# Output weights split during attention, output blocks handed out at 17 queued steps, and a VectorE that waits for GpSimd's power

## The chip, the cores and the metric

The kernel runs on one core of one Trainium2 chip. The metric is the device time of one execution in microseconds. The core has five engines with instruction streams of their own: TensorE (PE, the matmuls; its weight loads are counted apart as PEld), VectorE (DVE), ScalarE (ACT), GpSimd (POOL), and SyncE (SP), whose queue issues all the DMA transfers of this kernel, in order. Each engine runs its instructions in the order in which the program wrote them, and waits on semaphores for what the others make.

## The reference, cut to what matters

One decoder block, for one sequence of 1024 tokens and a width of 1024, in float32. The core of it:

```python
mod = silu(c) @ w_ada + b_ada              # six vectors: shift, scale, gate, twice
h = rms_norm(x, g_attn_pre) * (1 + sc_a) + sh_a
proj = h @ w_in                            # 1024 -> 2304 columns: qa, ka, va, qb, kb, vb
oa = banded_attention(...)                 # 8 heads, 2 key heads, window 128, with sinks
ob = dilated_mixture_attention(...)        # 8 heads, three dilated windows, mixed by softmax weight
mixed = concat(rms_norm(oa, g_mix_a), rms_norm(ob, g_mix_b))
y = mixed @ w_out                          # 1024 x 1024
x = x + gt_a * rms_norm(y, g_attn_post)
h = rms_norm(x, g_mlp_pre) * (1 + sc_m) + sh_m
y = square(relu(h @ w_up)) @ w_down        # 1024 -> 4096 -> 1024
x = x + gt_m * rms_norm(y, g_mlp_post)
```

## The kernel before, in words

**Products.** The large matmuls run in a rounded float32 format, fp32r. To keep the precision, each operand is split into a high part (the rounded value) and a low part (the value less the high part), and one product takes three matmuls: high by high, low by high, high by low. The splitting is elementwise work on ScalarE (the high part) and VectorE or GpSimd (the low part). One such group of three matmuls of 128 x 128 by 128 x 512 is called a dense step here.

**Stages.** (1) Modulation and normalization of x, whose result goes, split, into one large tile `hw` of 8 slots, each with a high and a low row of 1024 columns. (2) The input projection in six units u = 0 to 5 of two token halves x and three column tiles c; each tile has 8 dense steps, one for each 128 rows k of the weight (`proj_mm`, matmul lines L866, L867, L869). (3) Attention, in items of heads and token blocks: scores (L1127 and L1182), masked maximum (L1146, L1197), exponential (L1153, L1202), division by the sum (L1158 on GpSimd), transposes of the probabilities (L1232, L1235), splitting of the transposed probabilities on ScalarE and VectorE (L1246, L1250), the product with the values (L1262 to L1267, L1274), the values' own preparation (L836, L844, L847), and the store of an item's output to DRAM (L1301). Attention starts while the projections run and lasts some time after them. (4) The output projection in 8 blocks of 128 tokens (`out_block`, tb = 0 to 7): load the attention output `o_sb` (L1423), split it (L1436, L1439), compute the mixers' norms (L1441 to L1462), 16 dense steps with w_out (L1478 to L1480), post-norm, gate and residual (L1493 to L1524), the second norm, whose scaled result `xn` (L1532) is transposed on TensorE (`px`, L1541) and brought out as the MLP's input `h2` (L1557 on ScalarE, L1560 on VectorE). (5) The MLP in a Strassen-like scheme of seven block products for each half (`product`, matmuls L1912 to L1914), for which sums of weight blocks and of h2 blocks are made on VectorE (`sum_S` L1801, `sum_T` L1843) and split (L1667 to L1676).

**`hw` in turn.** The tile `hw` first holds the split activations, then the split w_out (a slot for each 128 rows k of w_out), then the operand pairs of the MLP. A slot can take w_out once the last projection tile that reads it is through. The counter `r_wo` stands for free slots. In the kernel before, k's 128 columns lie in all slots of a token half, so four slots come free together, at the end of a half's last tile (u = 5, c = 2).

**w_out.** `load_wo` does this for k = 0 to 7: a load of 128 x 1024 floats into one of five shared stage buffers (`wo_st`, L1348; the counter `r_stg`), the high part on ScalarE straight into `hw` (L1353), the low part on VectorE (L1356) or, in two instructions, on GpSimd (L1361, L1362), as the planner finds cheaper. The gate's row `gate_a` (L1377) and the buffers of the output blocks are made in the space of the stage buffers once those have been read.

**The order.** The order on each engine is not written by hand. A planner (`Sched`) builds it when the kernel is built: it keeps an estimated clock for each engine, a queue of steps for each, and for TensorE several streams ("s" scores, "t" transposes, "dense" and so on), with estimated durations, dependencies, priorities and counters of free buffers. It repeatedly takes the step that can start first. Feeders put steps into the queues when a condition holds: `feed_proj` keeps the dense stream filled with projection tiles, `feed_s` the attention items, `feed_out` hands out output blocks:

```python
if tb < TB and st.att >= 42 + 2 * (tb // 2) and len(sc.pe.get("dense", [])) <= 10:
    out_block(tb)
```

A step that can run on either of two engines names both. Once the order stands, the engines follow it, and what the chip needs beyond the estimates shows as waiting.

**The norms.** `norm(col, dep)` in `out_block` makes 1/sqrt(mean square + eps) of one column: VectorE scales and adds (L1515, tile `rs_t`), GpSimd raises it to the power -1/2 (L1517, tile `st`). Each block has two: one for the post-norm (col 0) and one for the MLP's pre-norm (col 2). ScalarE's `xn` waits for the second.

## Time and profile before

| | before |
|---|---|
| median of 3 runs | 1146.05 us (1145.21 to 1146.7) |
| the profiled execution's own time | 1144.1 us |
| its span, from first to last instruction | 1142.2 us |
| mean granted TensorE clock | 0.991 |
| TensorE busy | 1113.5 us, 97% |
| VectorE busy | 819.3 us, 72% |
| ScalarE busy | 636.1 us, 56% |
| GpSimd busy | 267.8 us, 23% |

The profile comes from one execution. Its rows give times in microseconds from the first instruction; an instruction row names its start, its length, the engine, the line of the kernel, the operation, its tiles (written <- read) and sizes, and in brackets the time that the engine sat idle before it with the instruction, on another engine or DMA, that released it. Matmuls overlap in the pipeline: a matmul that shows 0.39 us of length is followed by the next 0.23 us later. The granted clock is the share of TensorE's full speed that the chip allowed in a stretch. The projections run until 376.65 us, the first matmul of an output block stands at 397.86, the first of the MLP between the last output blocks (514.75 is one of them), and the MLP lasts to the end.

### The profile page before, as it was taken

To read this page: it belongs to the slowest core of one execution; us is meant where nothing else is said; L and a number is where in the kernel's file an instruction comes from. 1 tells how busy PE (TensorE), PEld (TensorE's weight loads), DVE (VectorE), ACT (ScalarE), POOL (GpSimd) and SP (SyncE) were. 2 spreads that over 40 slices of the span, in tenths; PEclk is the share of its full clock that TensorE was granted. 3 is DMA by queue.
4 is the path that set the end of the run, shared out by engine and by line. 5 is a ranking of instruction groups with operands and counts; after the bars stand their busy time and mean duration, and the time that the engine had idled before them with its cause. 6 is when DMAs were issued, how large, how long until landed. Compare 5 with 4: busy or idle time off the path is not lost.

```text
span 1142.2 us, 15600 instructions
## 1 busy us (share of the span) xinstructions
PE 1113.5 (97%) x5417; PEld 925.2 (81%) x5417; DVE 819.3 (72%) x1378; ACT 636.1 (56%) x1101; POOL 267.8 (23%) x349
## 2 busy tenths in 40 slices
PE   8999999999999899998999999999999999999996
PEld 7788878888888687887888888888888888888885
DVE  7878666666667766668879664599644896537998
ACT  8868865464556755676675434553244733246542
POOL 2458867565743521112000000000000000000002
PEclk9999999999999899999999999999999999999998
DMA  9565545343423305555780168712469112584103
GB/s 351 187 208 164 164 155 168 136 155 125 141 77 133 127 26 186 185 202 217 284 310 19 56 230 292 280 41 70 152 245 331 55 56 86 202 304 164 37 19 148
DMA packets 90910, 185.29 MB, mean 162 GB/s; under 512 B 8400, under 2 KB 31056, under 8 KB 90832
## 3 DMA queue, kind: packets, MB, share of 16 engines
q1 hardware_dynamic: 90832, 184.30, 46.1%
q8 instruction: 43, 0.70, 0.2%
q14 instruction: 35, 0.29, 0.1%
HBM read 137.08 MB, written 28.31 MB: 145 GB/s over the span
## 4 chain that ended last, share of the span: by engine, by line
PE 77%; DVE 8%; ACT 4%; issue 4%; POOL 3%; DMA 3%; SPq 0%; DVEq 0%; POOLq 0%; ACTq 0%
PE mlp_ps L1913 17%; PE mlp_ps L1914 17%; PE mlp_ps L1912 17%; PE pj L866 4%; PE pj L869 4%; PE pj L867 4%; PE s_ps L1127 3%; PE o_ps L1262 2%; PE y_ps L1478 1%; PE pt_ps L1232 1%; PE y_ps L1479 1%; PE y_ps L1480 1%; PE pt_ps L1235 1%; DMA o_sb<-o_dram 1%; PE o_ps L1267 1%
## 5 line engine op out<-in xcount | busy, mean ns | idle before, releaser
L1912 PE MATMUL mlp_ps<-hw 128*128 128x512 f32 x896 | 349.8, 390 | 0.0
L1913 PE MATMUL mlp_ps<-hw 128*128 128x512 f32 x896 | 348.8, 389 | 0.0
L1914 PE MATMUL mlp_ps<-hw 128*128 128x512 f32 x896 | 348.8, 389 | 0.0
L1912 PEld LDWEIGHTS mlp_ps<-hw 128*128 128x128 f32 x896 | 168.5, 188 | 35.5 <-issue 0.5
L1913 PEld LDWEIGHTS mlp_ps<-hw 128*128 128x128 f32 x896 | 168.4, 188 | 35.2 <-issue 0.5
L1914 PEld LDWEIGHTS mlp_ps<-hw 128*128 128x128 f32 x896 | 168.4, 188 | 34.9
L1676 DVE TENSOR_TENSOR hw<-w,hw 128x1024 fp32r<-128x1024 f32 x96 | 114.7, 1222 | 95.5 <-ACT hw L1669 95.2
L1669 ACT CAST hw<-w 128x1024 fp32r<-128x1024 f32 x96 | 97.7, 1047 | 128.1 <-PE mlp_ps L1914 97.5
L2012 POOL TENSOR_TENSOR st<-st,nhalf 128x1 f32<-128x1 f32 x8 | 7.8, 977 | 598.5 <-DVE st L2010 598.5
L866 PE MATMUL pj<-hw,w_hl 128*128 128x512 f32 x240 | 102.9, 429 | 0.0
L869 PE MATMUL pj<-hw,w_hl 128*128 128x512 f32 x240 | 95.1, 396 | 0.0
L867 PE MATMUL pj<-hw,w_hl 128*128 128x512 f32 x240 | 94.9, 395 | 0.0
L1250 DVE TENSOR_TENSOR ph<-pt_ps,ph 128x512 fp32r<-128x512 f32 (+1 forms) x110 | 69.5, 648 | 32.9 <-ACT ph L1246 32.6
L1669 ACT CAST hw<-u 128x1024 fp32r<-128x1024 f32 x48 | 48.6, 1051 | 64.6 <-PE mlp_ps L1914 64.6
L1246 ACT CAST ph<-pt_ps 128x512 fp32r<-128x512 f32 (+1 forms) x110 | 59.0, 556 | 31.2 <-PE pt_ps L1235 26.1
L1153 ACT ACTIVATE p_sb<-p_sb,mn 128x128 f32<-128x128 f32 (+3 forms) x64 | 49.7, 777 | 38.7 <-DVE mn L1146 37.2
L1676 DVE TENSOR_TENSOR hw<-u,hw 128x1024 fp32r<-128x1024 f32 x48 | 57.1, 1221 | 18.2 <-ACT hw L1669 18.2
L1970 DVE TENSOR_TENSOR yacc<-yacc,mlp_ps 128x512 f32<-128x512 f32 x96 | 62.3, 685 | 3.3 <-PE mlp_ps L1914 3.3
L1158 POOL TENSOR_SCALAR p_sb<-p_sb,den 128x128 f32<-128x128 f32 (+3 forms) x64 | 48.6, 765 | 55.4 <-DVE den L1156 50.8
L1015 POOL TENSOR_TENSOR ada_acc<-ada_acc,wa_st 128x512 f32<-128x512 f32 x42 | 54.9, 1307 | 3.5
L869 PEld LDWEIGHTS pj<-hw,w_hl 128*128 128x128 f32 x240 | 45.4, 189 | 10.6
L1478 PE MATMUL y_ps<-hw,oh 128*128 128x512 f32 x128 | 52.0, 406 | 0.0
(206 smaller groups left out, 2015.8 us busy)
## 6 DMA issues: line engine op xcount, KB each, us to landing
hw<-s_dram SPq DMA_DIRECT2D x84, 512.0 KB, 4.2
wa_st<-in_w_ada SPq DMA_DIRECT2D x32, 512.0 KB, 4.3
w<-in_w_up SPq DMA_DIRECT2D x32, 512.0 KB, 4.9
w<-in_w_down SPq DMA_DIRECT2D x32, 512.0 KB, 7.0
s_dram<-hw SPq DMA_DIRECT2D x28, 512.0 KB, 3.4
qt<-hl SPq DMA_DIRECT2D x40, 256.0 KB, 2.6
w_st<-in_w_in SPq DMA_DIRECT2D x36, 256.0 KB, 2.9
x_sb<-in_x SPq DMA_DIRECT2D x16, 512.0 KB, 6.5
```

The source lines that it names most:

```text
L866: T.matmul(ps, w[:, 0, n], h[0], start=(k == 0), stop=False)
L867: T.matmul(ps, w[:, 1, n], h[0], start=False, stop=False)
L869: T.matmul(ps, w[:, 0, n], h[1], start=False, stop=(k == KC - 1))
L1246: A.copy(b["ph"][:, 0, :w], b["pt"][:, :w])
L1250: V.tensor_tensor(b["ph"][:, 1, :w], b["pt"][:, :w], b["ph"][:, 0, :w].bitcast(F32), ALU.subtract)
L1478: T.matmul(ps[:], b["oh"][:, k], wh[:, c0:c0 + 512], start=(k == 4 * m), stop=False)
L1669: A.copy(out[j][0], flat(src[j]))
L1676: V.tensor_tensor(out[j][1], flat(src[j]), out[j][0].bitcast(F32), ALU.subtract)
L1912: T.matmul(ps[m][:], sh, mh, start=starts and k == 0, stop=False, **kw)
L1913: T.matmul(ps[m][:], sh, ml_, start=False, stop=False, **kw)
L1914: T.matmul(ps[m][:], sl, mh, start=False, stop=k == 3, **kw)
L1970: e = op("DVE", t_dv(512), lambda: V.tensor_tensor(y(), y(), ps[m][:], ALU.add), [e, ml.e_y[tb, n]], gives=gives, prio=1)
```

## The change

It has five parts.

1. The layout of `hw` during the projections: k's columns of a token half lie in one slot, 4x + k // 2, as 512 contiguous columns. A slot is free once the last projection tile has done an odd step k, and `r_wo` is given one by one.
2. The chunks 4 to 7 of w_out are split during attention (`split_wo`, called by `feed_wo` as the projections pass 2.2, 3.0, 3.8 and 4.6 units): load into a stage buffer, high part on ScalarE into a second stage buffer, low part on VectorE in place, and two stores of 512 KB to DRAM. `load_wo` later brings them into `hw` by eight loads of 512 KB without any splitting. It still splits the chunks 0 to 3 itself, with the low part always on VectorE.
3. `feed_out` hands out a block with up to 17 dense steps queued, before 10.
4. `norm`: the planner's estimate for the power is 0.55 instead of 1.2 us for blocks 0 to 5. For the second norm of block 7, the scaling (VectorE), the power (GpSimd) and a one-column copy on VectorE that reads the power's result are one step, so that VectorE does nothing else while GpSimd works.
5. `t.a = h2`: the MLP's first half refers to the dictionary of h2 tiles itself, not to a copy, so that its steps can be queued before all the tiles exist.

In the order that results, GpSimd has six w_out instructions fewer; VectorE has three more low parts and one copy; ScalarE has as many w_out passes as before; SP has 16 more DMA instructions; a few steps that two engines can do have changed sides. TensorE has the same 5417 matmuls, and the same number from the last projection matmul to the first of the MLP. The first matmul of an output block has 19 more attention instructions ahead of it. In block 7, VectorE makes the h2 tiles from px (L1560) before the last sums `sum_T` (L1843); in the kernel before one such sum stood ahead of them.

```diff
@@ -677,8 +677,8 @@
     def mod_chunk(k, eg, half):
         t0, t1 = (0, TB) if half is None else (4 * half, 4 * half + 4)
         n = (t1 - t0) * P
-        ks = slice(k * P, (k + 1) * P)
-        h, hh = xnT[:, k, t0 * P:t1 * P].rearrange("p (b t) -> p b t", t=P), hw[:, t0:t1, 0, ks]
+        h = xnT[:, k, t0 * P:t1 * P].rearrange("p (x t) -> p x t", t=512)
+        hh, hl = (hw[:, t0 // 4 * 4 + k // 2:t1 - 3 + k // 2:4, i, k % 2 * 512:k % 2 * 512 + 512] for i in range(2))
         deps = [eg] + (e_xn[0] + e_xn[1] if half is None else e_xn[half])
 
         def full(eng):
@@ -689,7 +689,7 @@
         eh = op("ACT", t_sb(n) + 2 * AP_COST, lambda: A.activation(hh, h, AF.Identity, bias=s_a[:, k:k + 1],
                                                                   scale=g_a[:, k:k + 1]), deps, prio=0)
         e = op("ACT", t_sb(n) + 2 * AP_COST, full(A), [eh], prio=0)
-        e = op("DVE", t_dv(n), lambda: V.tensor_tensor(hw[:, t0:t1, 1, ks], h, hh.bitcast(F32), ALU.subtract), [e],
+        e = op("DVE", t_dv(n), lambda: V.tensor_tensor(hl, h, hh.bitcast(F32), ALU.subtract), [e],
                prio=0)
         for x in (0, 1) if half is None else (half,):
             e_hh[k, x], e_hl[k, x] = eh, e
@@ -858,10 +858,9 @@
 
     def proj_mm(ps, u, c, k, x, part):
         i, n = w_at(u, c, k)
-        t, w = slice(k * P, (k + 1) * P), w_hl[u, i]
-        n = slice(n * P, n * P + P)
-        h = [hw[:, 4 * x:4 * x + 4, i, t] for i in range(2)]
-        ps = ps[:].rearrange("p (b t) -> p b t", t=P)
+        w, n = w_hl[u, i], slice(n * P, n * P + P)
+        h = [hw[:, 4 * x + k // 2, i, k % 2 * 512:k % 2 * 512 + 512] for i in range(2)]
+        ps = ps[:]
         if part != 1:
             T.matmul(ps, w[:, 0, n], h[0], start=(k == 0), stop=False)
             T.matmul(ps, w[:, 1, n], h[0], start=False, stop=False)
@@ -927,8 +926,8 @@
             gives = []
             if x and k % 4 == 3:
                 gives.append((r_w, 1))
-            if u == 5 and c == 2 and k == KC - 1:
-                gives.append((r_wo, 4))
+            if u == 5 and c == 2 and k % 2:
+                gives.append((r_wo, 1))
             d = dense(0.681, emit, [w_e[u, w_at(u, c, k)[0]]], takes=[(r_pj, 1)] if k == 0 else [], gives=gives, after=tick)
         evac(u, x, c, lambda: b[0], d, r_pj)
 
@@ -1336,13 +1335,46 @@
     NSTG2 = 4
     ph2 = Tok()
 
+    wo_dram = [[dram.tile([P, 1024], F32, name=f"wo_dram{k}_{i}") for i in range(2)] for k in range(4, KC)]
+    e_wod = {}
+
+    def split_wo(k):
+
+        raw, hi = [], []
+        g = cols[:, 56 + k:57 + k]
+
+        def f_l():
+            raw.append(stage("wo_st"))
+            nc.sync.dma_start(raw[0][:], w_out[k * P:(k + 1) * P])
+        e = load(f_l, 524288, takes=[(r_stg, 1)], prio=21)
+
+        def f_h():
+            hi.append(stage("wo_hi"))
+            A.mul(hi[0][:].bitcast(F32R), raw[0][:], g)
+        eh = op("ACT", t_sb(D) + AP_COST, f_h, [e], takes=[(r_stg, 1)], prio=9)
+
+        def f_lo():
+            V.scalar_tensor_tensor(raw[0][:].bitcast(F32R), raw[0][:], g, hi[0][:], ALU.mult, ALU.subtract)
+        el = op("DVE", t_dv(D) + AP_DV, f_lo, [eh], prio=9)
+        e_wod[k] = [load(lambda t=t, i=i: nc.sync.dma_start(wo_dram[k - 4][i][:], t[0][:]), 524288, [e_],
+                         gives=[(r_stg, 1)], prio=22) for i, (t, e_) in enumerate(((hi, eh), (raw, el)))]
+
+    def feed_wo():
+        k = 4 + len(e_wod)
+        if st.d > WO_AT[k - 4]:
+            split_wo(k)
+        return len(e_wod) == 4
+
+    WO_AT = (2.2, 3.0, 3.8, 4.6)
+    sc.launch.append(feed_wo)
+
     def load_wo():
 
-        if len(todo_dense) > 2 or ada.i < NADA:
+        if len(todo_dense) > 2 or ada.i < NADA or len(e_wod) < 4:
             return False
         ph2.e_wo, ph2.raw = {}, {}
         eh = None
-        for k in range(KC):
+        for k in range(4):
             def f_l(k=k):
                 ph2.raw[k] = stage("wo_st")
                 nc.sync.dma_start(ph2.raw[k][:], w_out[k * P:(k + 1) * P])
@@ -1356,12 +1388,12 @@
                 V.scalar_tensor_tensor(hw[:, k, 1], ph2.raw[k][:], g, hw[:, k, 0].bitcast(F32), ALU.mult,
                                        ALU.subtract)
             eh = op("ACT", t_sb(D) + AP_COST, f_h, [e] + ([eh] if eh else []), prio=4)
-
-            def f_lo2(k=k, g=g):
-                G.tensor_scalar(ph2.raw[k][:], ph2.raw[k][:], g, 1.0, ALU.mult, ALU.mult)
-                G.tensor_tensor(hw[:, k, 1], ph2.raw[k][:], hw[:, k, 0].bitcast(F32), ALU.subtract)
-            ph2.e_wo[k] = op(("DVE", "POOL"), (t_dv(D) + AP_DV, t_pts(D) + t_ptt(D)), (f_lo, f_lo2), [eh],
-                             gives=[(r_stg, 1)], prio=4)
+            ph2.e_wo[k] = op("DVE", t_dv(D) + AP_DV, f_lo, [eh], gives=[(r_stg, 1)], prio=4)
+        for k in range(4, KC):
+            def f_d(k=k):
+                for i in range(2):
+                    nc.sync.dma_start(hw[:, k, i].bitcast(F32), wo_dram[k - 4][i][:])
+            ph2.e_wo[k] = load(f_d, 1048576, e_wod[k], takes=[(r_wo, 1)], prio=-8, n=2)
         return True
 
     def open_out():
@@ -1398,7 +1430,7 @@
 
     def feed_out():
         tb = ph2.tb
-        if tb < TB and st.att >= 42 + 2 * (tb // 2) and len(sc.pe.get("dense", [])) <= 10:
+        if tb < TB and st.att >= 42 + 2 * (tb // 2) and len(sc.pe.get("dense", [])) <= 17:
             out_block(tb)
             ph2.tb += 1
         return ph2.tb == TB
@@ -1513,9 +1545,17 @@
                 t = small.tile([P, 8], F32, name="rs_t", tag="rs_t")
                 bx.append(t)
                 V.tensor_scalar(t[:, :1], b["st"][:, col:col + 1], 1.0 / D, EPS, ALU.mult, ALU.add)
-            e = op("DVE", 0.08, f1, [dep], prio=0)
-            return op("POOL", 1.2, lambda: G.tensor_tensor(b["st"][:, col + 1:col + 2], bx[0][:, :1], nhalf[:, :1],
-                                                            ALU.pow), [e], prio=0)
+            def f2():
+                G.tensor_tensor(b["st"][:, col + 1:col + 2], bx[0][:, :1], nhalf[:, :1], ALU.pow)
+            if tb < TB - 1 or col == 0:
+                e = op("DVE", 0.08, f1, [dep], prio=0)
+                return op("POOL", 0.55 if tb < TB - 2 else 1.2, f2, [e], prio=0)
+
+            def f3():
+                f1()
+                f2()
+                V.tensor_copy(bx[0][:, 1:2], b["st"][:, col + 1:col + 2])
+            return op("DVE", 0.95, f3, [dep], prio=0)
         e = op("ACT", t_sb(D) + AP_COST, f_sq(0, True), ey, prio=1)
         e = norm(0, e)
         e = op("DVE", t_dv(D), lambda: V.scalar_tensor_tensor(b["y"][:], b["y"][:], b["st"][:, 1:2], ph2.gate[:],
@@ -1720,7 +1760,7 @@
             fr.update({"T1": joins(r_raw, 2), "T3": joins(r_raw, 1), "B22": joins(r_raw, 3), "T4": joins(r_raw, 1),
                        "T2": joins(r_raw, 2)})
             if h == 0:
-                t.a = {q: h2[q] for q in h2}
+                t.a = h2
                 t.e_a = dict(e_h2)
                 t.ring = r_h2
                 t.new = ring_r
```

## The prediction

> **What bounds the kernel now.** I read the page's busy shares first, then the stretches by engine, then TensorE's waits in the stretches that are not full. Busy times by engine on the page:
>
> ```profile
> PE 1113.5 (97%) x5417; PEld 925.2 (81%) x5417; DVE 819.3 (72%) x1378; ACT 636.1 (56%) x1101; POOL 267.8 (23%) x349
> ```
>
> TensorE (PE) bounds the whole, and the change leaves its 5417 matmuls as they are. So it can win only where TensorE idles or runs below full clock. The stretches (columns: window, its length, busy us and count of PE, PEld, DVE, ACT, POOL, granted clock, DMA share, GB/s):
>
> ```profile
> 60.00:376.00 316.00, 312.19 (x1752) 262.85 (x1751) 215.61 (x573) 193.28 (x461) 199.65 (x258) 0.99 0.45 149
> 380.00:385.00 5.00, 3.42 (x23) 2.69 (x22) 3.94 (x13) 4.90 (x13) 2.27 (x4) 1.00 0.10 26
> 385.00:390.00 5.00, 4.16 (x28) 3.23 (x27) 4.95 (x11) 4.90 (x8) 3.30 (x2) 1.00 0.07 16
> 390.00:395.00 5.00, 3.12 (x13) 2.73 (x13) 4.39 (x13) 3.61 (x8) 4.92 (x4) 0.70 0.54 165
> 395.00:400.00 5.00, 4.60 (x20) 3.77 (x20) 3.65 (x10) 4.07 (x8) 3.12 (x4) 0.62 0.25 73
> 435.00:440.00 5.00, 3.49 (x21) 2.71 (x19) 2.37 (x5) 4.39 (x6) 0.55 (x1) 1.00 0.91 330
> 525.00:530.00 5.00, 4.40 (x20) 3.32 (x18) 5.00 (x7) 3.26 (x6) 3.51 (x1) 1.00 0.97 315
> 530.00:535.00 5.00, 2.69 (x11) 2.50 (x12) 2.21 (x6) 3.76 (x6) 1.08 (x1) 0.70 0.06 23
> 540.00:560.00 20.00, 20.00 (x90) 16.57 (x89) 19.97 (x20) 11.64 (x16) 0.00 (x0) 1.00 0.69 263
> ```
>
> From 60 to 376 us (projections with attention between them) TensorE lacks only 3.8 us. From 380 to 400 the projections have ended, and attention alone feeds it: ScalarE (ACT) is full, VectorE (DVE) nearly so, and TensorE idles 4.70 us and falls to a clock of 0.70 and 0.62. A second hole lies at 530 to 535, beside a VectorE that was full. From 540 on TensorE is full, and so is VectorE.
>
> TensorE's timeline (start, length, instruction, idle time before it and its releaser): two steps of the last projection tile, then the first hole up to the first matmul of an output block, L1478:
>
> ```profile
> 369.29 0.40 PE L869 MATMUL pj<-hw,w_hl 128*128 128x512 f32 x1
> ...
> 376.65 0.40 PE L869 MATMUL pj<-hw,w_hl 128*128 128x512 f32 x1
> ...
> 381.62 0.66 PE L836 MATMUL pv<-head,vt 128*128 128x128 f32 x4 [0.41 <-DVE ot L1298]
> 383.19 0.33 PE L1232 MATMUL pt_ps<-head,p_sb 128*128 128x128 f32 x1 [0.81 <-POOL p_sb L1158]
> 384.73 0.50 PE L1262 MATMUL o_ps<-ph,v_hl 128*128 128x256 f32 x2 [0.36 <-DVE v_hl L847]
> 387.13 0.38 PE L1262 MATMUL o_ps<-ph,v_hl 128*128 128x256 f32 x1 [0.81 <-DVE ph L1250]
> 390.56 0.39 PE L1262 MATMUL o_ps<-ph,v_hl 128*128 128x256 f32 x1 [0.56 <-ACT ph L1246]
> 392.27 0.58 PE L1262 MATMUL o_ps<-ph,v_hl 128*128 128x256 f32 x1 [1.32 <-DVE ph L1250]
> 396.45 0.47 PE L1232 MATMUL pt_ps<-head,p_sb 128*128 128x128 f32 x1 [0.40 <-POOL p_sb L1158]
> 397.86 0.78 PE L1478 MATMUL y_ps<-hw,oh 128*128 128x512 f32 x1
> ```
>
> What stands ahead of those releasers on their engines is the splitting of w_out. Its groups (count, shortest/median/longest ns, first and last start), and below them the VectorE and DMA-queue (SPq) rows of the same moment:
>
> ```profile
> L1353 ACT ACTIVATE hw<-wo_st,head x8: 1133/1139/1158, 351.0 to 388.4; 128x1024 fp32r<-128x1024 f32 x8
> L1356 DVE SCALAR_TENSOR_TENSOR hw<-wo_st,head,hw x5: 1276/1285/2481, 352.6 to 388.8; 128x1024 fp32r<-128x1024 f32 x5
> L1361 POOL TENSOR_SCALAR wo_st<-wo_st,head x3: 1127/1128/2090, 356.4 to 390.2; 128x1024 f32<-128x1024 f32 x3
> L1362 POOL TENSOR_TENSOR hw<-wo_st,hw x3: 2377/2383/2426, 357.6 to 392.4; 128x1024 fp32r<-128x1024 f32 x3
> ```
>
> ```profile
> 388.81 2.48 DVE L1356 SCALAR_TENSOR_TENSOR hw<-wo_st,head,hw 128x1024 fp32r<-128x1024 f32 x1
> ```
>
> ```profile
> 391.31 0.33 SPq L1377 DMA_DIRECT2D gate_a<-gate_d  x1
> 391.75 0.38 SPq L1423 DMA_DIRECT2D o_sb<-o_dram  x1
> ```
>
> The low halves made by VectorE and GpSimd (POOL) run until 392.4 + 2.38 = 394.8 there, and the first o_sb load, which the first output block needs, stands behind gate_a, whose buffer is one that the splits read.
>
> **Term A, the end of the projections.** Four of the eight splits leave this stretch: 4 x 1.14 = 4.6 us of ScalarE, two low halves of VectorE (1.28 + 2.48), two pairs of GpSimd (1.13 + 2.38, 2.09 + 2.38). In place of them stand eight 512 KB loads (term D). The idles whose releaser stood behind such an instruction are 0.81, 0.56, 1.32 and 0.40, together 3.09; the other three (0.41, 0.81, 0.36) I leave. The low clock cost 0.30 x 3.12 + 0.38 x 4.60 = 2.68 of TensorE's own time. Rows at full clock show 3.42 and 3.49 us busy of 5, rows at 0.70 show 3.12 and 2.69; with 3.09 us of idle gone the stretch lies above, so I count the clock as regained. A = 3.09 + 2.68 = 5.8. Ends: the stretch's full-speed work is 3.42 + 4.16 + 0.70 x 3.12 + 0.62 x 4.60 = 12.6, so 20 - 12.6 = 7.4 is the most; 2 is the least (1.32 and 0.81, the longest two) if the rest of attention sets the pace. The threshold of 17 instead of 10 puts no work in: it lets the o_sb loads of blocks 0 and 1 be issued together, and since 19 attention instructions more now stand ahead of the first L1478 on TensorE, it also could delay it; the sum is in these ends.
>
> By the Trainium skill, "TensorE: Matmul & The Clock Gate", Part 1, the clock is halved after at least one idle window of about 3.4 us; here it sank with no single gap above 1.32 us, so the trace differs from it. By that rule the short gaps would not be the cause, the 2.68 would stay, and the sum would be -8.3 instead of -11.0.
>
> **Term B, the output blocks.** TensorE's waits between 400 and 520:
>
> ```profile
> PE px L1541 <- ACT xn L1532: 1.5, 1, 1.5
> PE pm_o L1452 <- DVE rs_t L1515: 0.4, 1, 0.4
> ```
>
> Blocks handed out earlier have more dense steps (three matmuls each) queued between a block's normalization and its transposes. Of these 1.9 us I take 1.5, the px wait; the upper end is 1.9. A loss is not excluded, since the order on VectorE changes there: the lower end is one more idle like the 0.81 above, a loss of 0.8.
>
> **Term C, the last block's power.** GpSimd's, VectorE's and TensorE's rows around it, with an undisturbed block at 516.79 and the group of all powers:
>
> ```profile
> L1517 POOL TENSOR_TENSOR st<-rs_t,nhalf x16: 541/543/4592, 428.2 to 526.5; 128x1 f32<-128x1 f32 x16
> ```
>
> ```profile
> 516.79 1.03 PE L1541 MATMUL px<-head,xn 128*128 128x128 f32 x8
> 517.58 0.48 PE L1912 MATMUL mlp_ps<-hw 128*128 128x512 f32 x1
> ...
> 529.01 0.39 PE L1914 MATMUL mlp_ps<-hw 128*128 128x512 f32 x1
> 532.31 1.97 PE L1541 MATMUL px<-head,xn 128*128 128x128 f32 x8 [2.91 <-ACT xn L1532]
> 533.93 0.78 PE L1912 MATMUL mlp_ps<-hw 128*128 128x512 f32 x1
> ...
> 535.36 0.41 PE L1912 MATMUL mlp_ps<-hw 128*128 128x512 f32 x1
> ```
>
> One power of 16 took 4.59 us instead of 0.54, in the 5 us in which VectorE was busy 5.00, and TensorE stood 2.91 us for what follows it (power, xn, px). The change makes VectorE stand still behind the power, so nothing runs beside it on VectorE and I count 0.54. The power then ends 4.05 us sooner, and px could start at 532.31 - 4.05 = 528.26, before TensorE has done with the matmul of 529.01. So px follows that matmul by one matmul's pace (20.00/90 = 0.22), the next L1912 stands 0.79 later (517.58 - 516.79), at 530.02, and not at 533.93: 3.91. The three matmuls after it took 535.36 - 533.93 = 1.43 at the low clock against 3 x 0.22 = 0.67: 0.76 more. C = 4.67. For VectorE's standing I count 0.8, the power and half as much again for the hand-overs there and back. It is covered by this:
>
> ```profile
> 533.47 1.37 DVE L1560 TENSOR_SCALAR h<-px,g_m,s_m 128x128 f32<-128x128 f32 x4 [2.79 <-PE px L1541]
> ```
>
> VectorE idled 2.79 us for that px. Queued behind the new wait are the sums for the MLP's operands, and TensorE waits for those. Ends: 4.8, and 2, which is what is left if VectorE, full again from 540, passes 2.7 us of its idle time on to the products as a later start.
>
> **Term D, the eight reloads.** They go out as the hw slots come free, at each odd step of the last projection tile (369.29 is the first of them, 376.65 the last). Nearest row, loads of the same tile and size:
>
> ```profile
> hw<-s_dram SPq DMA_DIRECT2D x84, 512.0 KB, 4.2
> ```
>
> Two in flight end them by about 370 + 4 x 4.2 = 387, one at a time by 370 + 8 x 4.2 = 404. The first block's last chunks are wanted about 400 or later. I take 0; the end is the 404 case, some 4 us late. That hw's slots hold 512 contiguous columns instead of four strided pieces of 128 changes no count and no size; I take 0.
>
> **Term E, the splits made early.** Each is a load, one ScalarE pass (1.14), one VectorE pass (1.28; 2.48 beside GpSimd) and two stores. By the order of the changed program they run beside what now runs from about 145 to 295 us. Their cover is the dense projection work: 312.19 of 316. The one thin place there is the first split's:
>
> ```profile
> 145.02 0.68 DVE L762 TENSOR_TENSOR hl<-pj,tab 64x512 f32<-64x512 f32 x1 [4.90 <-POOL ada_acc L1015]
> ```
>
> ```profile
> 148.79 0.74 PE L1182 MATMUL s_ps<-kt,qt 128*128 128x256 f32 x4 [1.80 <-DVE mn L1197]
> ```
>
> There ScalarE gets 1.14 in front of the casts that TensorE's attention wants, and the SP queue's stores stand in order in front of the next loads while they wait for both halves. I take +1.0, one ScalarE pass nearly whole; the other three 0. Ends: -2 (the 1.80 wait falls away, as the planner reorders there) and 4 x (1.14 + 2.48) = 14.5, all of it in the open.
>
> By the Trainium skill, "SBUF — State Buffer", Who interferes with whom, a VectorE instruction with two SBUF inputs and a GpSimd one that reads SBUF cannot run together, and the one that came first keeps the port for its whole length. The trace agrees (2.48 against 1.28, 4.59 against 0.54), and it speaks against the early VectorE passes, since the row at 145.02 shows VectorE waiting 4.90 us for a busy GpSimd.
>
> **Sum.** -5.8 - 1.5 - 4.67 + 0 + 1.0 = -10.97. The profiled execution took 1144.1 us, which is 1.95 below the median of 1146.05; 1133.13 + 1.95 gives 1135.
>
> **Rivals.**
> 1. Attention's own chain sets the pace to 400 in any case (ACT 4.90 of 5 already at 380 to 385, when only one split was near): A is 2, the rest stands: -7.17, 1138.9. Against it: the four releasers named above stood behind splits.
> 2. The power's gain goes to VectorE: full at 525 to 530 and at 540 to 560, it is late by what it stood, and C falls to 2: -8.3, 1137.8. For it: 19.97 of 20. Against it: the 2.79 of idle time.
> 3. The reloads come one at a time: the first blocks stall about 4 us at 400, and A is spent. 404 - 400 = 4, so 1139. For it: one queue, issued in order. Against it: 330 GB/s in the 435 row.
> 4. Slower: the early splits are in the open. Each holds ScalarE, then VectorE, and the stores hold SP; all four whole cost 14.5 instead of 1.0: 1135 + 13.5 = 1148.5. It decides from (5.8 + 1.5 + 4.67) / 4 = 3.0 us each, of 3.62. For it: the waits at 145 and 148.79; against it: 312.19 of 316 is matmul, so that only a queue that runs dry shows.
> 5. The change doesn't do what it says: the power stays starved, or the px wait is set by another wait behind it (the first norm, y_sb). C is 0: 1139.8.
> 6. The clock sinks in that stretch for another reason than the short gaps, and the 2.68 stays: 1137.8. For it: no gap there is longer than 1.32. Against it: the two rows in which it sinks (3.12 and 2.69 us busy) are the ones with the least TensorE work. (It is what the Trainium skill's page on TensorE, cited under term A, would give.)
>
> **How the numbers follow.** Forecast 0.43; rivals 1, 2, 3, 5 and 6: 0.13, 0.08, 0.06, 0.06, 0.07; rival 4, 0.12; the last 0.05 goes to two or three of these shortfalls at once, ending near 1144 to 1148. I give 1135, the forecast. Its best ends (7.4 + 1.9 + 4.8 + 0) give 1132, and with the 2 us of term E 1130; the shortfalls alone reach 1139.8, rivals 1 and 5 together 1143.6. Range 1130 to 1144. A difference within 0.2% (2.3 us) can't be told here from no change. The forecast and rivals 1, 2, 3, 5 and 6 lie on the faster side, 0.83; of rival 4 (splits nearly whole in the open) and of the last case 0.03 each lies within 2.3 us, the other 0.11 above. Faster 0.83, same 0.06, slower 0.11.
>
> **What the changed profile would show.** A: the first matmul of an output block some 6 us earlier against the last projection matmul, and the clock at 1.00 from 385 to 400. B: no px idle above 0.5 before the MLP. C: no power above 1 us for the last block, and px without the 2.91. D: the hw loads landed before 390, no y_ps wait on DMA. E: 60 to 376 still 312 of 316, no wait on wo_st or wo_hi on TensorE's path. Wrong it is if the last projection matmul comes more than 4 us later than 376.65, or if the MLP's TensorE stretch, now full, shows idles on VectorE.

## The result, and the profile after

The changed kernel took 1135.42 us (median of 5 runs, 1134.65 to 1136.33). The kernel before took 1145.51 us (median of 5, 1144.73 to 1146.7). The ratio is 0.9918, with a 95% interval of 0.9906 to 0.993: some 9.4 us less. The forecast was 1135.0, from 1130 to 1144.

The profiled execution of the changed kernel took 1136.33 us, the longest of its five, and that of before 1144.1, which is under the shortest of the five timed runs. So the two traces stand 7.8 us apart, and the medians 10.1. The terms below are read between marks inside the traces, which leave out part of that: at the 100th projection matmul, ahead of the early splits, the changed kernel is already 0.9 us later (112.39 us before, 113.32 after). Over all the runs below that mark lies between 112.2 and 114.0.

Busy times on the page of the changed kernel:

```profile
PE 1109.7 (98%) x5417; PEld 920.9 (81%) x5417; DVE 819.1 (72%) x1377; ACT 635.7 (56%) x1103; POOL 254.1 (22%) x346
```

The stretches of the changed kernel (window, length, busy us and count of PE, PEld, DVE, ACT, POOL, granted clock, DMA share, GB/s):

```profile
60.00:376.00 316.00, 309.89 (x1735) 260.16 (x1734) 218.74 (x574) 196.10 (x461) 198.88 (x258) 0.99 0.50 166
380.00:385.00 5.00, 4.71 (x32) 4.09 (x30) 4.32 (x13) 4.06 (x10) 0.59 (x1) 1.00 1.03 413
385.00:390.00 5.00, 3.72 (x25) 3.18 (x26) 3.72 (x13) 3.92 (x11) 1.93 (x3) 1.00 0.86 311
390.00:395.00 5.00, 4.93 (x35) 3.99 (x33) 4.95 (x18) 4.04 (x10) 1.71 (x2) 1.00 0.11 31
395.00:400.00 5.00, 4.26 (x29) 3.47 (x28) 3.98 (x11) 4.93 (x9) 1.71 (x2) 1.00 0.76 231
430.00:460.00 30.00, 29.70 (x144) 24.17 (x143) 17.62 (x33) 18.48 (x30) 4.86 (x8) 1.00 0.41 139
530.00:535.00 5.00, 5.00 (x24) 4.14 (x23) 5.00 (x8) 3.10 (x7) 0.00 (x0) 1.00 0.70 281
535.00:540.00 5.00, 4.84 (x22) 3.69 (x21) 5.00 (x6) 4.83 (x7) 0.00 (x0) 1.00 0.99 311
```

From 380 to 400 TensorE idles 2.38 us instead of 4.70, at full clock instead of 0.70 and 0.62. The hole at 530 is gone. The projections, from 60 to 376, lack 6.1 us instead of 3.8.

TensorE's timeline of the changed kernel after the projections: the last projection matmul, the waits, the first output block.

```profile
380.15 0.40 PE L868 MATMUL pj<-hw,w_hl 128*128 128x512 f32 x1
...
385.12 0.66 PE L836 MATMUL pv<-head,vt 128*128 128x128 f32 x4 [0.41 <-DVE ot L1297]
386.69 0.33 PE L1231 MATMUL pt_ps<-head,p_sb 128*128 128x128 f32 x1 [0.81 <-POOL p_sb L1157]
388.22 0.51 PE L1261 MATMUL o_ps<-ph,v_hl 128*128 128x256 f32 x2 [0.35 <-DVE v_hl L847]
396.33 0.39 PE L1261 MATMUL o_ps<-ph,v_hl 128*128 128x256 f32 x1 [0.40 <-DVE ph L1249]
398.20 0.39 PE L1261 MATMUL o_ps<-ph,v_hl 128*128 128x256 f32 x1 [0.34 <-DVE ph L1249]
399.38 0.47 PE L1510 MATMUL y_ps<-hw,oh 128*128 128x512 f32 x1
```

The three waits that no split stood in front of are there still (0.41, 0.81, 0.35). Of the four that one did, 0.81, 0.56, 1.32 and 0.40, two of 0.40 and 0.34 are left. The last projection matmul comes 3.5 us later than before (376.65), and the first output block 19.2 us after it instead of 21.2 (397.86 - 376.65).

The last block's power, its px and the matmuls around it:

```profile
522.96 0.55 POOL L1549 TENSOR_TENSOR st<-rs_t,nhalf 128x1 f32<-128x1 f32 x1 [7.39 <-DVE rs_t L1547]
```

```profile
523.55 0.15 DVE L1557 COPY rs_t<-st 128x1 f32<-128x1 f32 x1 [0.66 <-POOL st L1549]
```

```profile
525.26 0.39 PE L1954 MATMUL mlp_ps<-hw 128*128 128x512 f32 x1
525.56 1.09 PE L1581 MATMUL px<-head,xn 128*128 128x128 f32 x8
526.41 0.48 PE L1952 MATMUL mlp_ps<-hw 128*128 128x512 f32 x1
```

The power takes 0.55 us, VectorE stands 0.66 for it, and px follows the matmuls with no named wait.

For the comparison of all runs I use four marks of TensorE in each trace: the 100th and the last of the 720 projection matmuls, the last of the 384 matmuls of the output blocks (L1478 to L1480 before), and the 150th of the MLP's. (The first of the MLP's, at 514.75 before, follows the last of the output blocks, at 514.52.) The three spans between them hold the early splits; the end of attention with the output blocks; and the last block's norm.

| | 100th to last projection matmul | to the last output block matmul | to the 150th MLP matmul | ratio to before, 95% |
|---|---|---|---|---|
| before | 264.3 | 137.9 | 40.4 | |
| changed | 266.8 | 130.5 | 36.5 | 0.9918 (0.9906 to 0.993) |
| no hold on VectorE | 266.0 | 130.4 | 39.8 | 0.9948 (0.9935 to 0.996) |
| before, with the norms | 263.5 | 138.5 | 36.6 | 0.9972 (0.9962 to 0.9981) |
| threshold 10 | 267.6 | 134.0 | 36.6 | 0.9957 (0.9944 to 0.9971) |
| all splits late | 264.8 | 137.9 | 36.6 | 0.9974 (0.9963 to 0.9985) |
| early from 2.5 units | 266.9 | 130.5 | 36.6 | 0.9909 (0.9891 to 0.9927) |
| early from 2.7 units | 266.7 | 130.4 | 36.5 | 0.9929 (0.9914 to 0.9944) |
| threshold 24 | 266.0 | 130.9 | 36.5 | 0.9933 (0.9919 to 0.9947) |
| before, with the layout | 265.4 | 140.7 | 40.3 | 1.002 (1.0009 to 1.003) |
| early, without the passes | 263.1 | 130.5 | 36.5 | 0.9898 (0.9885 to 0.9911) |
| early from 3.4 units | 268.2 | 130.6 | 36.6 | 0.9945 (0.9933 to 0.9958) |
| changed, old layout | 265.6 | 134.3 | 36.6 | 0.9961 (0.9949 to 0.9973) |
| early from 4.0 units | 266.3 | 130.6 | 36.6 | 0.9931 (0.9919 to 0.9944) |

Between the first two rows the spans give +2.6, -7.4 and -3.9, together -8.7 us. Among runs with the same work in a span the second and third columns agree within some 0.6 us; the first scatters by 1.6 (266.0 to 267.6 in the four runs with the changed kernel's early splits and layout).

The fifth part of the change (`t.a = h2`) has no run of its own. The third span is 36.6 without it (before, with the norms) and 36.5 with it, so nothing of the gain shows there.

### The profile page after: what moved, and what is told of

Its sections match the earlier page's. It is cut to its first block, busy times and chain, and to the rows that moved or that the text cites. A ratio compares the mean times of both kernels' runs of the same rounds, so it can differ in the third digit from the quotient of the medians.

```text
span 1134.6 us, 15647 instructions
## 1 busy us (share of the span) xinstructions
PE 1109.7 (98%) x5417; PEld 920.9 (81%) x5417; DVE 819.1 (72%) x1377; ACT 635.7 (56%) x1103; POOL 254.1 (22%) x346
## 4 chain that ended last, share of the span: by engine, by line
PE 78%; DVE 8%; POOL 4%; issue 3%; DMA 3%; ACT 2%; SPq 0%; DVEq 0%; POOLq 0%; ACTq 0%
PE mlp_ps L1952 16%; PE mlp_ps L1954 16%; PE mlp_ps L1953 16%; PE pj L865 3%; PE pj L866 3%; PE pj L868 3%; PE s_ps L1126 2%; PE y_ps L1510 2%; PE y_ps L1512 2%; PE y_ps L1511 2%; PE o_ps L1261 1%; DMA wo_st<-in_w_out 1%; POOL ada_acc L1014 1%; PE pt_ps L1231 1%; DVE hw L1716 1%
```

## The experiments

**The hold alone.** The copy is taken out; all engines keep their order.

```diff
                 f1()
                 f2()
-                V.tensor_copy(bx[0][:, 1:2], b["st"][:, col + 1:col + 2])
```

> The changed kernel without the one-column copy on VectorE behind the last block's power; everything else, the order on every engine included, stays, and the output is the same. Theory (VectorE's instructions beside the power starve it, and only VectorE's wait prevents it): the last power takes 3 to 4.6 us again instead of 0.55, TensorE waits 2 to 3 us for the last px, and the time is 1135.4 + 4 = 1139.4 us (1138 to 1140.5). Rival (the new order around the power did it, not the wait): the power stays near 0.55 to 1.5 us and the time within 1 us of 1135.4.

It took 1138.3 us, ratio 0.9948: 0.0030 of 1145, or 3.4 us, above the changed kernel. The power in this run, and TensorE's wait for what follows:

```profile
521.69 3.47 POOL L1549 TENSOR_TENSOR st<-rs_t,nhalf 128x1 f32<-128x1 f32 x1 [7.39 <-DVE rs_t L1547]
```

```profile
PE px L1580 <- ACT xn L1571: 2.0, 1, 2.0
```

What VectorE runs beside the power:

```profile
521.54 0.94 DVE L1840 TENSOR_TENSOR sum_S<-h,h 128x768 f32<-128x768 f32 x1
522.40 2.35 DVE L1715 TENSOR_TENSOR hw<-w,hw 128x1024 fp32r<-128x1024 f32 x2
```

One instruction of 0.15 us, with VectorE's stand of 0.66 us, makes the difference between a power of 0.55 and one of 3.47 us. The theory holds. The power ends at 525.16, 0.41 us after the last of these VectorE instructions (524.75); before, it ended 0.40 us after the last of four (531.08 and 530.68). The new order alone made the power a little shorter than before's 4.59, not short: one VectorE instruction fewer, a `sum_T` of 1.22 us, stands beside it.

**The norms alone**, on the kernel before:

```diff
-            return op("POOL", 1.2, lambda: G.tensor_tensor(b["st"][:, col + 1:col + 2], bx[0][:, :1], nhalf[:, :1],
-                                                            ALU.pow), [e], prio=0)
...
+                return op("POOL", 0.55 if tb < TB - 2 else 1.2, f2, [e], prio=0)
...
+            def f3():
+                f1()
+                f2()
+                V.tensor_copy(bx[0][:, 1:2], b["st"][:, col + 1:col + 2])
+            return op("DVE", 0.95, f3, [dep], prio=0)
```

> The kernel before with the part on the norms alone (VectorE waits for the last block's power; the planner's price of the other powers 0.55). Theory: the last power 0.55 us, no px wait of 2.9 us, 1145.5 - 4.3 = 1141.2 us (1140.5 to 1143). Rival (VectorE, full from 540 on, gives the gain back; or another wait stands behind it): 1144 to 1146.

The ratio is 0.9972, 3.2 us less than before; the third span is 36.6, as in the changed kernel. In the third span the gain is nearly the same without the rest of the change (3.8) as with it (3.3, by the run without the hold), so term C adds to the others.

**The threshold.**

```diff
-        if tb < TB and st.att >= 42 + 2 * (tb // 2) and len(sc.pe.get("dense", [])) <= 17:
+        if tb < TB and st.att >= 42 + 2 * (tb // 2) and len(sc.pe.get("dense", [])) <= 10:
```

> The changed kernel with blocks handed out at 10 queued dense steps as before. Theory (the late w_out splits made the hole at 380 to 400, and the threshold is worth the px wait of 1.5 us only): 1137 us, px idle of 1 to 1.5 us back in one block, clock still 1.00 from 380 to 400. Rival (the earlier loads of the attention output and the queued blocks closed the hole): 1140 to 1141 us with idle TensorE before the first output block. Second rival (the threshold does nothing): 1135.4.

The ratio is 0.9957, 4.5 us above the changed kernel (0.0039 of 1145); by the marks 134.0 against 130.5, 3.5 us. More than expected. TensorE in this run while the output blocks run, and its px wait:

```profile
430.00:460.00 30.00, 27.99 (x134) 22.62 (x133) 17.99 (x31) 17.97 (x29) 3.54 (x6) 1.00 0.53 179
```

```profile
PE px L1581 <- ACT xn L1572: 1.9, 1, 1.9
```

At a threshold of 17 the same 30 us hold 144 matmul records and 29.70 us of work, here 134 and 27.99. The hole from 380 to 400 stays as small as in the changed kernel, and its clock at 1.00: that part of the theory holds, and the rival that the threshold closed the hole falls.

**A threshold of 24** (`<= 24` in the same line):

> The changed kernel with blocks handed out at up to 24 queued dense steps instead of 17. Theory (at 17 no output block waits for its normalization any more: TensorE idles 0.3 us from 430 to 460): nothing left to gain, within 0.7 us of the changed kernel. Rival (the more steps are queued, the better): 1 us or more faster. Second rival (blocks handed out too early crowd VectorE and ScalarE out of the last attention items): slower by 1 us or more.

Ratio 0.9933, second span 130.9: no gain. The time is 1.7 us above the changed kernel, outside the expected 0.7, but the intervals overlap and the three spans together are no longer than the changed kernel's, so a loss is not shown. At 17 the blocks are early enough.

**All splits late.** The early splits and the reloads go, and `load_wo` splits all eight chunks as before:

```diff
-        for k in range(4):
+        for k in range(KC):
...
-            ph2.e_wo[k] = load(f_d, 1048576, e_wod[k], takes=[(r_wo, 1)], prio=-8, n=2)
+            ph2.e_wo[k] = op(("DVE", "POOL"), (t_dv(D) + AP_DV, t_pts(D) + t_ptt(D)), (f_lo, f_lo2), [eh],
+                             gives=[(r_stg, 1)], prio=4)
```

> The changed kernel with all eight chunks of w_out split at the end of the projections as before (VectorE or GpSimd for the low part), nothing stored to DRAM; layout, threshold of 17 and the norms of the changed kernel stay. Theory (term A comes from the late splits, term E is what the early ones cost): +5.8 and -2.6 (the projections' end 2.6 us earlier, which is what it came later in the changed kernel from 198 us on and at the first split), 1138.6 us (1137.5 to 1140), low clock and 3 us or more of idle between 380 and 400. Rival (the threshold closed the hole): 1132.8 us.

1141.41 us, ratio 0.9974: 6.4 us above the changed kernel, and not 3.2. The projections come back by 2.0 (264.8 against 266.8), but the second span grows by 7.4, to 137.9: as expected TensorE idles again behind the projections, longest 2.47 us, and works at half the clock from 384.92 to 395.16. The rival, that the threshold closed the hole, falls here too.

**The layout alone**, on the kernel before: the first part of the change and nothing else (cut to its counter).

```diff
-            if u == 5 and c == 2 and k == KC - 1:
-                gives.append((r_wo, 4))
+            if u == 5 and c == 2 and k % 2:
+                gives.append((r_wo, 1))
```

> The kernel before with the new layout of hw alone, and w_out's slots counted free one by one. Theory: no change, ratio 1.000 within 0.001. Rival (the late splits start earlier, one slot at a time, and crowd the last projection steps, as the run with all eight splits late hints, whose projections took 1.4 us longer at their end): 1 us slower or more.

Ratio 1.002 (1.0009 to 1.003): slower by some 2.3 us. The theory of no change falls. The rival's price holds, its place only in part: the projections take 1.1 us more, which is within their scatter, and the second span is 140.7, 2.8 longer than before's. TensorE in this run, and the stretches after its longest wait:

```profile
383.40 0.27 PE L1234 MATMUL pt_ps<-head,p_sb 128*128 128x128 f32 x1
386.13 1.12 PE L836 MATMUL pv<-head,vt 128*128 128x128 f32 x4 [2.46 <-DVE ot L1297]
```

```profile
383.53 2.21 DVE L1355 SCALAR_TENSOR_TENSOR hw<-wo_st,head,hw 128x1024 fp32r<-128x1024 f32 x1 [0.36 <-ACT hw L1352]
385.67 0.41 DVE L1297 TENSOR_TENSOR ot<-o_ps,otmp 64x256 f32<-64x256 f32 x1
```

```profile
385.00:390.00 5.00, 3.87 (x16) 3.53 (x16) 4.58 (x12) 4.06 (x10) 3.99 (x4) 0.55 0.39 118
390.00:395.00 5.00, 4.45 (x21) 4.24 (x20) 3.67 (x11) 1.99 (x5) 0.12 (x1) 0.50 0.12 30
```

A late split's low part stands on VectorE ahead of the instruction (`ot`) that frees what TensorE waits for; TensorE stands 2.46 us and works ten microseconds at about half the clock. With slots counted free one by one, the order that the planner makes puts late splits in front of other attention steps than before, and worse ones.

So the second span adds up: 140.7 with the layout alone; 137.9 with the layout, the threshold and the norms (-2.8); 134.0 with the layout, the early splits and the norms (-6.7); 130.5 with all, 0.7 less than the two steps alone would give.

**The old layout in the changed kernel**, the same edit the other way round:

> The changed kernel with the old layout of hw, so that four slots of w_out come free together at the end of a half's last tile; all else stays. Theory (the reloads have slack): they start some 5 us later, at the last projection matmul, end before 395, and the first output block waits little: 0 to 2 us slower, ratio 0.992 to 0.9935. Rival (the layout costs by itself, as the run with the layout alone hints, which was 2.4 us slower than before): 2 us faster, ratio 0.990.

Ratio 0.9961: 4.9 us slower than the changed kernel, 3.8 of it in the second span. That is more than the 0 to 2 us of the theory, and the rival, a gain of 2 us, falls: beside the early splits the layout helps, and by itself it costs. The first reload and the first output block of this run:

```profile
378.60 4.00 SPq L1396 DMA_DIRECT2D hw<-wo_dram  x8
```

```profile
404.20 0.39 PE L1511 MATMUL y_ps<-hw,oh 128*128 128x512 f32 x1
```

In the changed kernel the reloads go out in two groups, and the first output block starts 19.2 us after the last projection matmul (399.38 - 380.15), here 25.8 (404.20 - 378.41):

```profile
374.92 1.99 SPq L1395 DMA_DIRECT2D hw<-wo_dram  x4
377.00 0.70 SPq L1300 DMA_DIRECT2D o_dram<-ot  x1
378.03 3.11 SPq L1395 DMA_DIRECT2D hw<-wo_dram  x4
```

The reloads' median time to landing in the changed kernel is 6.4 us, so the last, issued by 381.1, were there by about 388, 11 us before they were wanted. In the run with the old layout they were issued by 382.6 and would have been in time too. Its late first block comes with another planned order rather than from a wait for these loads: 134 of TensorE's matmuls stand between the last projection matmul and the first output block instead of 111, and TensorE idles 5.0 us there instead of 2.4. The longest of these waits is for `ot` again:

```profile
393.59 0.48 PE L1262 MATMUL o_ps<-ph,v_hl 128*128 128x256 f32 x2 [1.63 <-DVE ot L1298]
```

VectorE makes this `ot` at 393.03, more than 5 us after ScalarE's copy for it was ready (387.58), since other attention steps stand before it; in the changed kernel that distance is 1.2 us (389.31, 390.47). What the rest of the order costs I did not separate.

**Where the early splits stand.** `WO_AT` is the list of units at which they are handed out.

```diff
-    WO_AT = (2.2, 3.0, 3.8, 4.6)
+    WO_AT = (2.5, 3.1, 3.8, 4.6)
```

> The changed kernel with the early splits handed out at 2.5, 3.1, 3.8 and 4.6 units instead of 2.2, 3.0, 3.8 and 4.6, so that the load of the first no longer waits for the stage buffer that GpSimd holds, with ScalarE standing behind it. Theory (most of term E is ScalarE's wait for that load): the wait of 2.5 to 2.7 us of TensorE near 150 us vanishes, the projections end 1.5 to 2 us earlier, ratio to before 0.990 to 0.9905, about 1.6 us under the changed kernel. Rival (each of the four splits costs its share wherever it stands): no change against the changed kernel, another wait in its place.

> The same with 2.7, 3.2, 3.9 and 4.6 units: the first split in the denser attention of the later units. Theory: as with 2.5, 1.5 to 2 us under the changed kernel; the three later splits keep about 1 us of cost among them. Rival: with less room between them, the splits cost more than in the run with 2.5.

> The changed kernel with the early splits at 3.4, 4.0, 4.5 and 5.0 units, where GpSimd has little left to do. Theory (each pass costs TensorE about 0.7 us wherever attention runs beside it): no change against the changed kernel, the projections end at 379.5 to 380.5. Rival (it is the crowd of the adaLN work on GpSimd and of the first units that makes them dear): 1.5 us or more faster, ratio 0.990.

> The same as the run at 3.4 to 5.0 with 4.0, 4.4, 4.8 and 5.2 units, so that the splits come closer together. Theory: as there, no change, since the price goes with the passes; if each waits for the one before, up to 1 us slower. Rival: 1.5 us or more faster than the changed kernel.

The wait that the first of these was made for is plain in the changed kernel. ScalarE stands idle for the load of the first chunk, with casts of attention queued behind it, and TensorE stands for those casts:

```profile
145.95 0.35 SPq L1348 DMA_DIRECT2D wo_st<-in_w_out  x1
```

```profile
149.59 1.15 ACT L1353 ACTIVATE wo_hi<-wo_st,head 128x1024 fp32r<-128x1024 f32 x1 [5.06 <-DMA wo_st<-in_w_out]
150.64 0.60 ACT L768 CAST hl<-hl 128x512 fp32r<-128x512 f32 x1
```

```profile
152.51 0.50 PE L1273 MATMUL o_ps<-ph,v_hl 128*128 128x512 f32 x1 [2.73 <-ACT ph L1245]
```

With 2.5 units, TensorE's waits from 140 to 200 us are these:

```profile
PE s_ps L1181 <- DVE mn L1196: 1.8, 1, 1.8
PE o_ps L1273 <- ACT ph L1245: 1.1, 1, 1.1
PE o_ps L1273 <- DVE ph L1249: 0.9, 1, 0.9
```

The 2.73 is gone, and the 1.8 that the kernel before had at 148.79, and that the new order had removed, is back, with 1.1 and 0.9 beside it. The first span is 266.9, as in the changed kernel. At 2.7 and 4.0 units it is 266.7 and 266.3, at 3.4 it is 268.2. The theory that the wait for the one load is most of the price falls; the rival, another wait in its place, holds for all four lists: the longest waits in the projections are 2.7 us at 2.7 units, 2.4 at 3.4 and 1.9 at 4.0. The run at 3.4 units was slower by 3 us than the changed kernel, against what was expected. That at 4.0 was slower by 1.5, with overlapping intervals. The ratio of 0.9909 at 2.5 units is within the interval of the changed kernel's 0.9918, and its marks are the same: it is no better version.

**Without the passes.** The early chunks are loaded and stored, but ScalarE and VectorE do nothing to them:

```diff
         def f_h():
-            hi.append(stage("wo_hi"))
-            A.mul(hi[0][:].bitcast(F32R), raw[0][:], g)
+            hi.append(raw[0])
...
         def f_lo():
-            V.scalar_tensor_tensor(raw[0][:].bitcast(F32R), raw[0][:], g, hi[0][:], ALU.mult, ALU.subtract)
+            pass
```

> The changed kernel without the four early passes on ScalarE and the four on VectorE: the loaded chunks are stored to DRAM as they are, both times, so four chunks of w_out are used unsplit and unscaled and the output is another; loads, stores, reloads and the planned order of all other instructions stay. Theory (term E, 2.9 us in the runs so far wherever the early splits stand, is the passes' time on ScalarE and VectorE among attention's casts): the projections end 2.5 to 3 us earlier, 1132.5 us, ratio 0.989. Rival (it is the loads and stores in the SP queue, or the order that the planner made around the splits): within 1 us of the changed kernel, ratio 0.9918.

Ratio 0.9898, 2.3 us under the changed kernel; the projections take 263.1, 3.7 us less than there and no more than before. All the other spans are the changed kernel's. The two ratios' intervals overlap a little (up to 0.9911, from 0.9906), so the size is rough, but the projections say the same: 265.6 to 268.2 in the nine runs with early passes, 263.1 to 265.4 in the five without. So the loads, the 8 MB of stores and reloads and the order cost nothing that shows here, and the price of the early splits is the passes themselves, with what ScalarE and VectorE stand for them, among attention's work on these engines.

## Why the prediction was right, point by point

The total was right (-11.0 forecast against -9.4 by the ratio and -10.1 by the medians), in part by luck. Between the marks the terms come to -3.9 - 3.5 - 3.9 + 2.6 = -8.7: A and C were 2.7 too large together, B was 2.0 too small, which nearly cancels, and E was 1.6 too cheap. That the median came within 0.5 us of 1135.0 is chance besides: the forecast added 1.95 us because the profiled execution of before lies that much below its median, and that of the changed kernel lies 0.9 above its own.

- **Term A, the end of the projections: 5.8 forecast, 3.9 found** (137.9 before against 134.0 with the threshold at 10), inside the ends of 2 to 7.4. The mechanism was right: the splits stood in front of VectorE's and ScalarE's casts, and with them gone the clock stays at 1.00. From 380 to 400 the low clock goes whole, and the idle time falls by 2.32 (4.70 to 2.38), not 3.09. The step that failed is taking the four idles whole: two waits of 0.40 and 0.34 for `ph` are in their place, on attention's own chain. Over the whole second span TensorE idles 1.9 less (7.6 to 5.7) and is busy 2.0 less (130.3 to 128.2). The layout goes into this 3.9 as well, and it isn't free: against the run with the layout alone (140.7) the run with the threshold at 10 is 6.7 shorter, so the 3.9 is a gain and a loss together. The sign given for A came only in part: the first output block is 2.0 us earlier against the last projection matmul, not 6, with 19 more attention instructions ahead of it.
- **Term B, the output blocks: 1.5 forecast, 3.5 found** (134.0 against 130.5), and 2.8 where the splits were late (140.7 against 137.9, with the norms' new price in it). The bound of 1.9 was too low, though it holds all but 0.1 us of the idle time that before has from 430 to 460:

```profile
430.00:460.00 30.00, 27.99 (x134) 22.60 (x133) 18.49 (x35) 15.95 (x25) 4.89 (x6) 1.00 0.51 178
```

```profile
439.13 1.09 PE L1541 MATMUL px<-head,xn 128*128 128x128 f32 x8 [1.51 <-ACT xn L1532]
449.64 0.58 PE L1452 MATMUL pm_o<-ones,o_sb 128*128 128x1 f32 x4 [0.42 <-DVE rs_t L1515]
```

  From the first output block matmul to the last, at a threshold of 10 and of 17:

```profile
399.65:514.37 114.72, 111.37 (x563) 91.92 (x562) 74.87 (x139) 74.35 (x119) 17.59 (x26) 1.00 0.44 151
399.38:510.63 111.25, 110.20 (x564) 91.87 (x563) 73.88 (x139) 73.21 (x119) 17.45 (x26) 1.00 0.44 151
```

  The idle time falls from 3.35 to 1.05, by 2.3; where the splits were late it falls by 1.9 (2.95 to 1.08), as the named waits say. The rest, 1.2, is TensorE's busy time, shorter for the same matmuls. A stop costs more than the idle time shown in front of it, since the matmul ahead of it runs out its 0.39 us where the next would have come after 0.23: at a threshold of 10, px comes 2.26 us after the matmul before it (438.90 - 436.64) and shows 1.88 of idle. That is a part of the 1.2; the rest is not separated. The term was mis-sized by pricing stops as idle time, and by taking the waits of before for those of the new order.
- **Term C, the power: 4.67 forecast, 3.9 between the traces, 3.3 and 3.8 in the two runs that separate it.** px came 0.30 after the last matmul (525.56 - 525.26) where I had 0.22, and the next matmul 0.85 later where I had 0.79. By the 96th MLP matmul 4.3 us were gained; from there to the 150th, 0.5 went back: VectorE is busy 5.00 of 5 from 530 to 540, and TensorE 4.84 in the second half, with one wait of 0.16 us for VectorE. That is rival 2 at a fifth of its price.
- **Term D, the reloads: 0 forecast, and right.** They landed some 11 us ahead. Its other half, the layout at 0, was wrong twice over: alone it costs 2.8 us in the second span, and the changed kernel without it is slower by 3.8 there. I had looked at the instructions that the layout changes, which are the same in count and size, and not at what freeing the slots one by one does to the order.
- **Term E, the early splits: 1.0 forecast, 2.6 found between the traces, 2.3 to 3.7 by the run without the passes.** The place was right: the first split's pass, with ScalarE standing 5.06 us for its load. The step that failed is costing the other three at 0 behind a full TensorE, and the first at one pass. TensorE is full on average there, but its order is fixed; a cast that comes late stops it although matmuls of the projection stand behind. The signs given for E did not come: 60 to 376 holds 309.9 us of TensorE's work and not 312, and the wait on `wo_st` was on TensorE's path, by way of ScalarE. The last projection matmul came 3.5 us later, close to the 4 that would have meant the term was wrong. At some 0.6 to 0.9 us for each split, rival 4 (3.6 each) was far off.
- **Rival 1** holds in part (A is smaller, not 2). **Rival 3** and **rival 5** fall: the reloads were there in time and the power is short. **Rival 6** falls: the clock stayed at 1.00 from 380 to 400 in every run with the early splits, and fell there in every run with the late ones. So in this kernel the 2.68 us did hang on them, against the rule of the Trainium skill's page "TensorE: Matmul & The Clock Gate", Part 1, that I had set beside it, read as one idle gap of about 3.4 us: the longest gap there was 2.47 us. How the gaps add up stands in the last section.

## What to carry to other kernels

Where a fixed order feeds the bounding engine, elementwise work put beside it need not be free just because that engine is full: here each split cost 0.6 to 0.9 us, a quarter to two fifths of its two passes' length. Test by leaving out the pass and keeping its transfers. Bound what a change can win from the elapsed time of a stretch against its matmuls at their undisturbed pace, and count the low clock with it; the idle time of named waits is only a part. A counter that frees buffers sooner changes a planned order, and its price must be sought there and not in the instructions it touches.

## What the runs showed of the hardware that I had not expected

- The power on one column of 128 x 1 took 0.55 us with VectorE at rest and 3.47 and 4.59 us while VectorE ran one instruction with two SBUF operands after another. By the Trainium skill, "SBUF — State Buffer", Who interferes with whom, the one that comes second is blocked for the whole of the other's instruction; the longest of those here took about 1.2 us, so in these traces GpSimd was held up over several of them, until the last had ended. That was starving, and a stand of 0.66 us on VectorE ended it.
- TensorE's clock fell by what TensorE did in a stretch of 3.41 us, not by the length of one gap. Before, it fell at 149.67, 392.02 and 531.96, whole multiples of 3.41 us apart, and stayed at half for 3.41, 6.83 and 3.41 us; in the two runs with the late splits and the new layout it stayed there for 10.24. In the fourteen traces it fell 15 times between 80 and 1100 us, each time after a stretch of 3.41 us in which TensorE was busy 0.85 to 1.75 us by the profile's rows, about half at most. In stretches of that length laid back to back from a fall, it never fell after one with 1.85 us or more, and not after all of those with 1.55 to 1.75. Rows of before, of the run with all splits late, and of the run with the old layout:

```profile
388.61:392.02 3.41, 1.74 (x9) 0.96 (x7) 3.41 (x5) 3.04 (x6) 3.41 (x2) 1.00 0.07 16
392.02:398.85 6.83, 6.18 (x23) 5.33 (x24) 4.96 (x18) 4.83 (x10) 5.10 (x5) 0.50 0.58 174
```

```profile
381.51:384.92 3.41, 1.66 (x9) 1.10 (x8) 3.05 (x7) 3.36 (x8) 3.33 (x3) 1.00 0.00 1
384.92:395.16 10.24, 8.71 (x37) 8.17 (x38) 8.44 (x23) 5.88 (x14) 4.21 (x5) 0.50 0.24 72
```

```profile
392.48:395.90 3.42, 2.01 (x16) 1.81 (x16) 1.54 (x6) 2.10 (x5) 1.71 (x2) 1.00 0.08 19
```

  So gaps of at most 1.32 us brought it down together, while a wait of 2.75 us in the run at 2.7 units, which lay across two such stretches, left it at 1.00.
